# Second norm's channel weights moved from w_up to the normalised rows, the rows' scale given priority on GpSimd, and the values' two parts summed by one reduction from PSUM

## The chip, the cores and the metric

The kernel runs on one core of a Trainium2 chip. Its engines are TensorE (PE in the profile, with its weight loads as PEld), VectorE (DVE), ScalarE (ACT), GpSimd (POOL) and SyncE (SP), which issues the DMAs. The metric is the time of one execution in microseconds (us); a row's durations are in us unless marked ns.

## The reference

One layer of a hybrid decoder, on 1024 tokens of 1024 channels with 16 meta tokens ahead of them:

```python
def rms_norm(x, g):
    xf = x.astype(jnp.float32)
    y = xf * lax.rsqrt(jnp.mean(xf * xf, axis=-1, keepdims=True) + EPS)
    return (y * g.astype(jnp.float32)).astype(x.dtype)
...
        hn = rms_norm(h, norm1_gain[l])
        proj = jnp.einsum('bld,de->ble', hn, w_in[l])
...
        mixed = jnp.concatenate([attn_out, conv_out], axis=-1)
        h = h + jnp.einsum('ble,ed->bld', mixed, w_out[l])
        hn = rms_norm(h, norm2_gain[l])
        a = jax.nn.relu(jnp.einsum('bld,df->blf', hn, w_up[l]))
        h = h + jnp.einsum('blf,fd->bld', a * a, w_down[l])
    return h[:, N_META:]
```

`proj` holds queries, keys and values of 4 heads and the input of a convolution group. The attention is causal and differential: for each head `a = p[0] - lam * p[1]`, two softmax maps of 64-wide queries and keys, times values of 128 columns, and an RMS norm of each head's result. `w_up` is 1024 x 4096, `w_down` 4096 x 1024, all in float32.

## The kernel before

**Exact products out of parts.** Every float32 operand of a matrix product is split into a high part, rounded to fp32r, and a low part, the remainder. The helpers `split` and `halves` do it: ACT copies the high part, and DVE (or GpSimd, where `eng` says so) subtracts it from the source. `three` (L319 to L321) then makes a product of three matmuls, high x high, high x low, low x high. Nearly all of TensorE's work goes through it, so a line of the profile such as `px<-hnt,wp` is told by its tile.

**Stages.** From 0 to 20 us x is loaded, normalised and transposed; to 240 us the projections of the convolution, keys and queries run, with the convolution's taps on DVE; to 480 us the attention, the values, and the output product; to about 530 us the rest of the output product and the second norm; to 820 us the up stage; then the down stage.

**The attention's values.** `values(i, h, u)` runs for each of 8 tiles of 128 queries and 4 heads. For each block of keys, one matmul multiplies the weights' high part with the value's high and low part side by side (256 columns of a PSUM tile `ops`), and one adds the weights' low part times the value's high part to the left 128. The two halves of `ops` are then added: ACT copies the right one to `ob` (L623), DVE adds the left one to it, into `osb` (L624).

**The second norm.** `attn_out` adds the output product to the residual into `hs` (or `h2k`, for the tiles that stay in SBUF) and sums its squares. When both halves of a tile of 128 rows are there, two GpSimd operations make the row's scale: `ms` (L698, sum and epsilon) and `rs2` (L699, power -1/2; `rs` in the profile). `normed(t)` multiplies the rows by that scale on DVE (`xn`, L832), 512 columns at a time, and TensorE transposes them into PSUM (`htr`, L835). The channel weights of the norm are not applied there but to the rows of `w_up` when these are loaded (`wload`): by ACT for each load of 128 x 4 x 256 (L894, four instructions), by GpSimd for the first eight, of 128 x 4 x 128 (L892). They lie in SBUF as `gains`, one column for each block of 128 channels.

**The up stage.** It multiplies blocks of 2 x 2 with seven products in place of eight. So the transposed rows are needed in seven forms: `hn11`, `hn21`, `hn22` and the sums and differences `hnt1` to `hnt4`, made by `norm_first`, `norm_second` and `norm_third`, the last in halves of 256 columns (`hnt` in the profile; `scr` and `hraw` hold what they are made of). The weights have seven forms too, made by `up_prep(g)`: sums `s1`, `s2` on DVE out of two loads `wr`, then parts `wp`. `group(g)` runs for 16 blocks of 256 columns of `w_up`; in it `snap` copies a product from PSUM to `sn` on ACT (L941), after which TensorE goes on accumulating into the same bank. The first four groups begin early, while the norm still runs: `up_early` multiplies `hn11` and `hn21` with parts made by `prep_early`, whose low parts GpSimd makes. 

**What sets the order.** The program is written out by hand; a scheduler then orders the instructions of each engine by the program's order, its own model of times and the priorities (`tc.high_priority`). An engine works through its own list in order. All DMAs of the lines below are issued on SP's queue, in order as well.

Of the kernel before, what the change touches and what calls it, by code (L numbers as in the profile page):

```python
# [9 lines left out]
F32 = mybir.dt.float32  # L10
# [49 lines left out]
def hybrid_layer_kernel(  # L60
# [36 lines left out]
    def small(shape, name, bufs=2):  # L97
        return sp.tile(shape, F32, tag=name, name=name, bufs=bufs)
# [62 lines left out]
    xm = cp.tile([P, 8, 48], F32R, tag="xm", name="xm")  # L161
# [67 lines left out]
    V.tensor_scalar(gsub, cvec[:, 0, 3:4], (1.0 - 0.2) * P ** 0.5, None, ALU.mult)  # L229

# [381 lines left out]
    def values(i, h, u):  # L612
# [10 lines left out]
        S.activation(ob, ops[:, P:2 * P], AF.Copy)  # L623
        V.tensor_tensor(out=osb[:, h, :], in0=ops[:, 0:P], in1=ob, op=ALU.add)  # L624
# [59 lines left out]
    def attn_out(pool, t, nh, keep=None):  # L684

        if keep is None:
            hs = tmp([P, 512], F32, "hs")
        else:
            hs = keep.tile([P, 512], F32, tag="ut", name="h2k", bufs=UT)
            h2t.setdefault(t, []).append(hs)  # L690
        nc.sync.dma_start(hs, cvo[t, nh])
        ps = half_out(pool, ma, state[0, nh], t)
        V.tensor_tensor(out=hs, in0=hs, in1=ps, op=ALU.add)
        nc.sync.dma_start(h2d[t][:, 512 * nh:512 * nh + 512], hs)
        S.activation(ps, hs, AF.Square, scale=D ** -0.5, accum_out=ssq[:, t, nh:nh + 1])
        if nh:
            ms = small([P, 8], "ms", 4)[:, :1]
            G.tensor_scalar(ms, ssq[:, t, 0:1], ssq[:, t, 1:2], EPS, ALU.add, ALU.add)  # L698
            G.tensor_tensor(out=rs2[:, t:t + 1], in0=ms, in1=mhalf[:, :1], op=ALU.pow)  # L699
# [51 lines left out]
    for n in range(-1, len(units) + BLAG):  # L751
# [12 lines left out]
        if n == 1:  # L764
            st_pool.__exit__(None, None, None)
            yt_pool.__exit__(None, None, None)
            aux_pool = tc.tile_pool(name="aux", bufs=1, side="right", reuse_waits="tile")
# [53 lines left out]
    def normed(t):  # L821
# [8 lines left out]
        for kf in range(2):  # L830
            xn = sp.tile([P, 512], F32, tag="raw", name="xn", bufs=4)
            V.tensor_scalar(xn, hv[kf], rs2[:, t:t + 1], None, ALU.mult)  # L832
# [34 lines left out]
    def norm_third():  # L867

        for name in ("t4", "t1", "t3"):
            operand(name)  # L870
            for c in (256, 0):
# [6 lines left out]
                elif name == "t1":  # L878
                    halves(hi, lo, t1)
# [7 lines left out]
    def wload(g, j, n):  # L887
# [3 lines left out]
        if n == P:  # L891
            G.tensor_tensor(out=r, in0=r, in1=gains[:, 1, 4 * j:4 * j + 4].unsqueeze(2).broadcast_to([P, 4, P]), op=ALU.mult)  # L892
        for k in range(4) if n > P else ():
            S.activation(r[:, k, :], r[:, k, :], AF.Copy, scale=gains[:, 1, 4 * j + k:4 * j + k + 1])  # L894
# [204 lines left out]
    up_pool.__exit__(None, None, None)  # L1099
    ps_c.__exit__(None, None, None)  # L1100
# [136 lines left out]
```

## Time and profile before

| what | value |
|---|---|
| median of 3 runs | 1135.59 us (1133.06 to 1140.71) |
| profiled execution | 1135.33 us, span 1133.2 us |
| PE | 1098.8 us busy, 97% of the span |
| DVE | 817.2 us, 72% |
| ACT | 617.1 us, 54% |
| POOL | 149.2 us, 13% |

The span is the time from the first to the last instruction in the trace; the profiled execution's time is measured around it. A busy share counts an engine's instructions over the whole span. It doesn't say which engine is waited for: that is read from the waits, the idle time of an instruction just before it starts and what ended it. The granted clock (PEclk) is the share of its full speed that TensorE had; 0.5 is the lower of its two levels, 1.2 GHz, and 1.0 the upper, 2.4 GHz.

### The profile page before, as it was taken

How to read it: one execution, taken by the hardware profiler on the slowest of the kernel's cores; microseconds unless marked ns; L12 is line 12 of the kernel's file. 1: busy time of each engine (PE TensorE's matmuls, PEld its weight loads, DVE VectorE, ACT ScalarE, POOL GpSimd, SP SyncE). 2: the span in 40 equal slices, each digit the busy share in tenths (PEclk: the TensorE clock that was granted, in tenths of full speed). 3: DMA queues.
4: the chain of work that ended last, by engine and by line, in shares of the span. 5: the costliest groups of instructions: out<-in, count | busy, mean ns of one | idle time of the engine just before them, and what ended most of it. 6: DMA issues, size and time to landing. Idle time of an engine off the chain costs nothing.

```text
span 1133.2 us, 15762 instructions
## 1 busy us (share of the span) xinstructions
PE 1098.8 (97%) x5696; PEld 925.5 (82%) x5696; DVE 817.2 (72%) x1354; ACT 617.1 (54%) x1378; POOL 149.2 (13%) x160
## 2 busy tenths in 40 slices
PE   6999999999999999898999999999999999999998
PEld 6999788877788887786888877888878888888887
DVE  7699899977888788689688868787656545356340
ACT  7521465447667677568767667767555333323320
POOL 3000564313001351261000000000000000000000
PEclk9999999999999999998999999999999999999999
DMA  7420011100213411365489989879399675565600
GB/s 266 121 76 1 1 38 38 29 10 19 75 66 103 131 66 66 122 224 170 154 309 330 323 277 343 320 251 339 125 336 380 251 258 212 197 227 201 221 38 37
DMA packets 89309, 191.23 MB, mean 169 GB/s; under 512 B 7552, under 2 KB 28288, under 8 KB 83600
## 3 DMA queue, kind: packets, MB, share of 16 engines
q1 hardware_dynamic: 89232, 190.24, 48.0%
q8 instruction: 44, 0.72, 0.3%
q14 instruction: 33, 0.27, 0.1%
HBM read 130.44 MB, written 59.77 MB: 168 GB/s over the span
## 4 chain that ended last, share of the span: by engine, by line
PE 72%; DVE 10%; DMA 8%; ACT 5%; issue 3%; POOL 1%; SPq 0%; DVEq 0%; ACTq 0%; POOLq 0%
PE py L319 6%; PE py L320 6%; PE py L321 6%; PE px L321 5%; PE px L319 5%; PE px L320 5%; DMA wr<-in_w_up 3%; PE pu L319 3%; PE pu L320 3%; PE pu L321 3%; DMA wdr<-in_w_down 3%; PE pq L320 3%; PE pq L319 3%; PE pq L321 3%; PE ops L620 2%
## 5 line engine op out<-in xcount | busy, mean ns | idle before, releaser
L809 DVE TENSOR_TENSOR pair<-rv,pair 128x2048 fp32r<-128x2048 f32 x56 | 127.0, 2289 | 112.0 <-ACT pair L808 111.8
L808 ACT ACTIVATE pair<-rv 128x2048 fp32r<-128x2048 f32 x56 | 105.2, 1911 | 163.2 <-PE py L321 77.9
L319 PE MATMUL py<-pair 128*128 128x512 f32 x256 | 99.6, 389 | 0.0
L320 PE MATMUL py<-pair 128*128 128x512 f32 x256 | 99.6, 389 | 0.0
L321 PE MATMUL py<-pair 128*128 128x512 f32 x256 | 99.6, 389 | 0.0
L319 PE MATMUL px<-pair 128*128 128x512 f32 x192 | 74.8, 390 | 1.0 <-ACT pair L808 1.0
L320 PE MATMUL px<-pair 128*128 128x512 f32 x192 | 74.7, 389 | 0.0
L321 PE MATMUL px<-pair 128*128 128x512 f32 x192 | 73.8, 390 | 0.2 <-DVE pair L809 0.2
L320 PE MATMUL pu<-xT,w 128*128 128x260 f32 x256 | 72.4, 286 | 0.0
L321 PE MATMUL pu<-xT,w 128*128 128x260 f32 x256 | 71.7, 285 | 0.0
L319 PE MATMUL pu<-xT,w 128*128 128x260 f32 x256 | 71.7, 286 | 0.0
L894 ACT ACTIVATE wr<-wr,gains 128x256 f32<-128x256 f32 x128 | 55.0, 498 | 30.6 <-DMA wr<-in_w_up 29.7
L945 ACT ACTIVATE a<-a 128x512 f32<-128x512 f32 x60 | 36.9, 626 | 35.9 <-DVE a L812 24.6
L321 PEld LDWEIGHTS py<-pair 128*128 128x128 f32 x256 | 48.1, 188 | 10.0
L319 PEld LDWEIGHTS py<-pair 128*128 128x128 f32 x256 | 48.1, 188 | 9.9
L320 PEld LDWEIGHTS py<-pair 128*128 128x128 f32 x256 | 48.1, 188 | 9.9
L319 PE MATMUL px<-hnt,wp 128*128 128x512 f32 x128 | 50.5, 395 | 3.9 <-ACT sn L941 3.9
L321 PE MATMUL pq<-w,xT 128*128 128x512 f32 x128 | 50.9, 398 | 0.0
L319 PE MATMUL pq<-w,xT 128*128 128x512 f32 x128 | 50.9, 397 | 0.0
L320 PE MATMUL pq<-w,xT 128*128 128x512 f32 x128 | 50.8, 397 | 0.0
L320 PE MATMUL px<-hnt,wp 128*128 128x512 f32 x128 | 50.4, 394 | 0.4 <-DVE hnt L809 0.4
L321 PE MATMUL px<-hnt,wp 128*128 128x512 f32 x128 | 50.5, 394 | 0.0
(301 smaller groups left out, 3197.6 us busy)
## 6 DMA issues: line engine op xcount, KB each, us to landing
rv<-as SPq DMA_DIRECT2D x28, 1024.0 KB, 6.3
wr<-in_w_up SPq DMA_DIRECT2D x32, 512.0 KB, 5.2
as<-a SPq DMA_DIRECT2D x64, 256.0 KB, 5.4
wdr<-in_w_down SPq DMA_DIRECT2D x8, 2048.0 KB, 9.5
ws<-wdr SPq DMA_DIRECT2D x32, 512.0 KB, 4.5
rv<-ws SPq DMA_DIRECT2D x16, 1024.0 KB, 4.8
as<-as SPq DMA_DIRECT2D x48, 256.0 KB, 4.1
rv<-in_w_down SPq DMA_DIRECT2D x12, 1024.0 KB, 6.6
```

What stands on the lines that cost most here:

```text
L319: T.matmul(ps, st[0], mv[0], start=first, stop=False, skip_group_check=more)
L320: T.matmul(ps, st[0], mv[1], start=False, stop=False, skip_group_check=more)
L321: T.matmul(ps, st[1], mv[0], start=False, stop=last, skip_group_check=more)
L620: T.matmul(ops, u[:, 0, b, :], vb.rearrange("p a e -> p (a e)"), start=b == 0, stop=False)
L808: S.activation(hi, src, AF.Copy)
L809: (eng or V).tensor_tensor(out=lo, in0=src, in1=hi.bitcast(F32), op=ALU.subtract)
L894: S.activation(r[:, k, :], r[:, k, :], AF.Copy, scale=gains[:, 1, 4 * j + k:4 * j + k + 1])
L945: S.activation(c, c, AF.Relu)
```

## The change

```diff
@@ -158,7 +158,7 @@
 
 
 
-    xm = cp.tile([P, 8, 48], F32R, tag="xm", name="xm")
+    xm = wpool[0].tile([P, 8, 48], F32R, tag="xm", name="xm", bufs=1)
     G.memset(xm.bitcast(F32), 0.0)
     mraw = slot([NMETA, D], F32, "mraw")
     nc.sync.dma_start(mraw, meta)
@@ -227,6 +227,10 @@
     V.tensor_scalar(lnh[:, 1, :], cvec[:, :, 2], 0.5, None, ALU.mult)
     gsub = cp.tile([P, 1], F32, tag="gsub", name="gsub")
     V.tensor_scalar(gsub, cvec[:, 0, 3:4], (1.0 - 0.2) * P ** 0.5, None, ALU.mult)
+
+
+    grow = dr.tile([8, P], F32, tag="grow", name="grow")
+    nc.sync.dma_start(grow.rearrange("k p -> p k"), gains[:, 1, :])
 
     gq = tmp([P, HD], F32, "gq")
     gk = tmp([P, HD], F32, "gk")
@@ -620,8 +624,7 @@
             T.matmul(ops, u[:, 0, b, :], vb.rearrange("p a e -> p (a e)"), start=b == 0, stop=False)
             T.matmul(ops[:, 0:P], u[:, 1, b, :], vb[:, 0, :], start=False, stop=b == i + 1)
         ob = ap.tile([P, P], F32, tag="ob", name="ob")
-        S.activation(ob, ops[:, P:2 * P], AF.Copy)
-        V.tensor_tensor(out=osb[:, h, :], in0=ops[:, 0:P], in1=ob, op=ALU.add)
+        V.tensor_reduce(osb[:, h, :], ops.rearrange("p (a e) -> p e a", a=2), axis=AX.X, op=ALU.add)
         S.activation(ob, osb[:, h, :], AF.Square, accum_out=oss[:, h:h + 1])
 
     def finish(i, osb, oss):
@@ -694,9 +697,10 @@
         nc.sync.dma_start(h2d[t][:, 512 * nh:512 * nh + 512], hs)
         S.activation(ps, hs, AF.Square, scale=D ** -0.5, accum_out=ssq[:, t, nh:nh + 1])
         if nh:
-            ms = small([P, 8], "ms", 4)[:, :1]
-            G.tensor_scalar(ms, ssq[:, t, 0:1], ssq[:, t, 1:2], EPS, ALU.add, ALU.add)
-            G.tensor_tensor(out=rs2[:, t:t + 1], in0=ms, in1=mhalf[:, :1], op=ALU.pow)
+            with tc.high_priority():
+                ms = small([P, 8], "ms", 4)[:, :1]
+                G.tensor_scalar(ms, ssq[:, t, 0:1], ssq[:, t, 1:2], EPS, ALU.add, ALU.add)
+                G.tensor_tensor(out=rs2[:, t:t + 1], in0=ms, in1=mhalf[:, :1], op=ALU.pow)
 
     uqs, pend = [], []
     for t in range(NT):
@@ -764,6 +768,9 @@
         if n == 1:
             st_pool.__exit__(None, None, None)
             yt_pool.__exit__(None, None, None)
+            gain_pool = tc.tile_pool(name="gain", bufs=1, side="right", reuse_waits="tile")
+            gain2 = gain_pool.__enter__().tile([P, D], F32, tag="gain2", name="gain2")
+            nc.sync.dma_start(gain2, grow.rearrange("k p -> (k p)").partition_broadcast(P))
             aux_pool = tc.tile_pool(name="aux", bufs=1, side="right", reuse_waits="tile")
             aux = aux_pool.__enter__()
             ap2 = tc.tile_pool(name="ap2", bufs=2, reuse_waits="tile")
@@ -829,7 +836,7 @@
         banks = []
         for kf in range(2):
             xn = sp.tile([P, 512], F32, tag="raw", name="xn", bufs=4)
-            V.tensor_scalar(xn, hv[kf], rs2[:, t:t + 1], None, ALU.mult)
+            V.scalar_tensor_tensor(xn, hv[kf], rs2[:, t:t + 1], gain2[:, 512 * kf:512 * kf + 512], ALU.mult, ALU.mult)
             bank = pcm.tile([P, 4, P], F32, tag="mm", name="htr")
             for q in range(4):
                 T.transpose(bank[:, q, :], xn[:, q * P:(q + 1) * P], ident)
@@ -876,7 +883,7 @@
                     sub(V, r21, t2, r21)
                     halves(hi, lo, r21)
                 elif name == "t1":
-                    halves(hi, lo, t1)
+                    halves(hi, lo, t1, G)
                 else:
                     sub(V, t2, t2, r11)
                     halves(hi, lo, t2)
@@ -888,10 +895,6 @@
 
         r = up.tile([P, 4, n], F32, tag="wr", name="wr", bufs=WRB, padded_shape=[P, 4, 256])
         nc.sync.dma_start(r, w_up[512 * j:512 * j + 512, 256 * g:256 * g + n].rearrange("(k p) f -> p k f", p=P))
-        if n == P:
-            G.tensor_tensor(out=r, in0=r, in1=gains[:, 1, 4 * j:4 * j + 4].unsqueeze(2).broadcast_to([P, 4, P]), op=ALU.mult)
-        for k in range(4) if n > P else ():
-            S.activation(r[:, k, :], r[:, k, :], AF.Copy, scale=gains[:, 1, 4 * j + k:4 * j + k + 1])
         return r
 
     def wpair(g, n, v, eng=None):
@@ -1097,6 +1100,7 @@
             next(run[g])
     next(run[NG - 1])
     up_pool.__exit__(None, None, None)
+    gain_pool.__exit__(None, None, None)
     ps_c.__exit__(None, None, None)
     tr_pool.__exit__(None, None, None)
```

Four things change. (a) The scaling of the loads of `w_up` by `gains` is gone from ACT and GpSimd. In its place `xn` is made by one SCALAR_TENSOR_TENSOR on DVE, with the row's scale and with `gain2`, a tile that holds the 1024 channel weights in each of the 128 partitions. `gain2` is loaded by one broadcasting DMA from `grow`, a row in DRAM, which an earlier DMA writes out of `gains`, transposing it. (b) The two GpSimd operations for the row's scale have a high priority. (c) The low parts of `hnt1` are made on GpSimd. (d) The two halves of `ops` are added by one TENSOR_REDUCE of DVE, which reads PSUM with the two values of a sum 128 columns apart; the copy `ob` on ACT goes (ACT still squares the result into it). `xm` moves to another pool.

GpSimd, the last operations that it has in the program, before; `wr` and `wp` are the early groups' loads and parts, `ms` and `rs2` the row's scale:

```order
L892 TENSOR_TENSOR wr_6294<-wr_6294,gains_106 128x4x128
L699 TENSOR_TENSOR rs2_2665<-ms_6191,mhalf_87 128x1
L892 TENSOR_TENSOR wr_6320<-wr_6320,gains_106 128x4x128
L892 TENSOR_TENSOR wr_6326<-wr_6326,gains_106 128x4x128
L809 TENSOR_TENSOR wp_6291<-wr_6288,wp_6291 128x512
L809 TENSOR_TENSOR wp_6297<-wr_6294,wp_6297 128x512
L698 TENSOR_SCALAR ms_6253<-ssq_2664 128x1
L809 TENSOR_TENSOR wp_6323<-wr_6320,wp_6323 128x512
L699 TENSOR_TENSOR rs2_2665<-ms_6253,mhalf_87 128x1
L809 TENSOR_TENSOR wp_6329<-wr_6326,wp_6329 128x512
```

And with the change:

```order
L816 TENSOR_TENSOR wp_6261<-wr_6259,wp_6261 128x512
L816 TENSOR_TENSOR wp_6266<-wr_6264,wp_6266 128x512
L702 TENSOR_SCALAR ms_6162<-ssq_2666 128x1
L703 TENSOR_TENSOR rs2_2667<-ms_6162,mhalf_87 128x1
L702 TENSOR_SCALAR ms_6224<-ssq_2666 128x1
L703 TENSOR_TENSOR rs2_2667<-ms_6224,mhalf_87 128x1
L816 TENSOR_TENSOR wp_6291<-wr_6289,wp_6291 128x512
L816 TENSOR_TENSOR wp_6296<-wr_6294,wp_6296 128x512
L816 TENSOR_TENSOR hnt1_6470<-scr_6165,hnt1_6470 128x4x256 x2
```

The scalings are gone, the last two pairs of `ms` and `rs2` stand together ahead of the last two parts, and the two halves of `hnt1` come at the end.

ACT in the up stage, around an `sn` of a group past the first four, before; `wr_7803` and `wr_7809` are the two loads from which this group's parts `wp` come, `wr_7983` is the second load of the next, `a11` and `a21` are results:

```order
L808 ACTIVATE wp_7815<-wr_7803 128x512
L946 ACTIVATE a11_7755<-a11_7755 128x512
L945 ACTIVATE a21_7771<-a21_7771 128x512
L946 ACTIVATE a21_7771<-a21_7771 128x512
L894 ACTIVATE wr_7983<-wr_7983,gains_106 128x256 x2
L941 ACTIVATE sn_7801<-px_7727 128x512
L808 ACTIVATE wp_7818<-wr_7809 128x512
L894 ACTIVATE wr_7983<-wr_7983,gains_106 128x256 x2
```

The same place with the change, where the group's own loads are `wr_7698` and `wr_7700`:

```order
L948 ACTIVATE a11_7650<-a11_7650 128x512
L949 ACTIVATE a11_7650<-a11_7650 128x512
L815 ACTIVATE wp_7702<-wr_7698 128x512
L948 ACTIVATE a21_7666<-a21_7666 128x512
L949 ACTIVATE a21_7666<-a21_7666 128x512
L944 ACTIVATE sn_7696<-px_7622 128x512
L815 ACTIVATE wp_7705<-wr_7700 128x512
L815 ACTIVATE wp_7712<-s2_7709 128x512
```

Two scalings of the next group's second load stood ahead of `sn` and two behind it. Now only results and a part made from the group's own first load stand ahead, and no instruction of this piece reads the next group's loads.

DVE at the end of the second norm, from the last pair of `xn`, before; `scr` and `hraw` lead to the parts of `hnt1`, `hnt2` and `hnt4`:

```order
L832 TENSOR_SCALAR xn_6422<-h2k_6217,rs2_2665 128x512
L832 TENSOR_SCALAR xn_6429<-h2k_6235,rs2_2665 128x512
L809 TENSOR_TENSOR hnt4_6512<-hraw_5914,hnt4_6512 128x4x256
L809 TENSOR_TENSOR hnt1_6519<-scr_6194,hnt1_6519 128x4x256
L812 TENSOR_TENSOR scr_6194<-htr_6411,scr_6194 128x4x128
L812 TENSOR_TENSOR scr_6194<-htr_6424,hraw_5914 128x4x128
L815 TENSOR_TENSOR s1_6376<-wr_6364,wr_6370 128x512
L812 TENSOR_TENSOR scr_6194<-htr_6431,scr_6194 128x4x128
L812 TENSOR_TENSOR s2_6377<-s1_6376,wr_6364 128x512
L812 TENSOR_TENSOR wr_6364<-wr_6364 128x4x128
L812 TENSOR_TENSOR hraw_5914<-scr_6194,hraw_5914 128x4x256
L815 TENSOR_TENSOR s1_6395<-wr_6383,wr_6389 128x512
```

And with the change:

```order
L839 SCALAR_TENSOR_TENSOR xn_6373<-h2k_6188,rs2_2667,gain2_3418 128x512
L839 SCALAR_TENSOR_TENSOR xn_6380<-h2k_6206,rs2_2667,gain2_3418 128x512
L819 TENSOR_TENSOR scr_6165<-htr_6278,scr_6165 128x4x128
L819 TENSOR_TENSOR hraw_5889<-scr_6165,hraw_5889 128x4x256
L816 TENSOR_TENSOR hnt2_6166<-scr_6165,hnt2_6166 128x4x128
L819 TENSOR_TENSOR scr_6165<-htr_6355,hraw_5889 128x4x128
L816 TENSOR_TENSOR hn22_6167<-htr_6278,hn22_6167 128x4x128
L819 TENSOR_TENSOR scr_6165<-scr_6165,hraw_5889 128x4x256
L816 TENSOR_TENSOR hnt4_6463<-hraw_5889,hnt4_6463 128x4x256
L819 TENSOR_TENSOR scr_6165<-htr_6362,scr_6165 128x4x128
L819 TENSOR_TENSOR scr_6165<-htr_6375,hraw_5889 128x4x128
L816 TENSOR_TENSOR wp_6339<-s2_6336,wp_6339 128x512
```

The part of `hnt1` is gone from behind the last `xn`, the sums `s1` and `s2` of the first early group have gone ahead of them, and in their place stand the sums of an earlier tile.

DVE in the up stage with the change, where the sums `s1_7874` and `s2_7875` read the next group's two loads directly; `as` are sums of the group's results:

```order
L816 TENSOR_TENSOR wp_7702<-wr_7698,wp_7702 128x512
L822 TENSOR_TENSOR as1_7670<-a21_7666,a22_7602 128x512
L822 TENSOR_TENSOR s1_7874<-wr_7864,wr_7866 128x512
L819 TENSOR_TENSOR as2_7671<-as1_7670,a11_7484 128x512
L819 TENSOR_TENSOR a21_7666<-a11_7484,a21_7666 128x512
L819 TENSOR_TENSOR s2_7875<-s1_7874,wr_7864 128x512
L819 TENSOR_TENSOR wr_7864<-wr_7864 128x4x128
L819 TENSOR_TENSOR as4_7672<-a12_7587,as2_7671 128x512
```

`s1_7874` stands behind the first of the group's four sums `as`; before, it stood behind the fourth and behind one part `wp`.

## Rows read from the trace of the kernel before

**Rows 1.** Windows by stage: from and to, us, busy time and instructions by engine, PEclk, DMA

```profile
20.00:240.00 220.00, 220.00 (x1380) 196.02 (x1379) 199.71 (x369) 90.58 (x389) 58.24 (x37) 1.00 0.15 44
240.00:480.00 240.00, 228.87 (x1443) 193.08 (x1442) 187.43 (x460) 165.29 (x428) 56.50 (x73) 1.00 0.22 75
480.00:530.00 50.00, 44.81 (x216) 36.72 (x216) 44.35 (x62) 37.68 (x78) 25.03 (x24) 0.93 0.62 205
530.00:820.00 290.00, 286.05 (x1253) 235.87 (x1252) 225.62 (x336) 201.62 (x393) 0.00 (x0) 0.99 0.79 276
```

**Rows 2.** Waits of TensorE: for which line, us in total, times, longest us

```profile
PE htr L835 <- DVE xn L832: 4.7, 2, 4.4
PE px L319 <- ACT sn L941: 3.9, 2, 2.8
...
PE ops L620 <- DVE osb L624: 1.2, 2, 0.7
```

**Rows 3.** Costliest groups of the page: busy us, mean ns, idle before and its releaser

```profile
L894 ACT ACTIVATE wr<-wr,gains 128x256 f32<-128x256 f32 x128 | 55.0, 498 | 30.6 <-DMA wr<-in_w_up 29.7
```

**Rows 4.** Timeline of ACT in the up stage: start, duration, then idle before

```profile
681.77 0.91 ACT L894 ACTIVATE wr<-wr,gains 128x256 f32<-128x256 f32 x2 [1.24 <-DMA wr<-in_w_up]
```

**Rows 5.** Timeline of TensorE at the same place

```profile
683.21 0.50 PE L319 MATMUL px<-hnt,wp 128*128 128x512 f32 x1 [2.79 <-ACT sn L941]
...
684.48 0.60 PE L321 MATMUL px<-hnt,wp 128*128 128x512 f32 x1
...
688.12 0.39 PE L321 MATMUL px<-hn,wp 128*128 128x512 f32 x1
```

**Rows 6.** GpSimd's groups by form between 489 and 528.1 us

```profile
L809 POOL TENSOR_TENSOR wp<-wr,wp 128x512 fp32r<-128x512 f32 x8 | 10.7, 1355 | 0.1
L892 POOL TENSOR_TENSOR wr<-wr,gains 128x512 f32<-128x512 f32 x8 | 8.5, 1075 | 8.5 <-PE htr L835 7.1 <-DVE hn L809 1.3
```

**Rows 7.** Timeline of GpSimd at the last tile of the norm

```profile
512.85 1.54 POOL L699 TENSOR_TENSOR rs<-ms,mhalf 128x1 f32<-128x1 f32 x1
```

**Rows 8.** Timeline of DVE from there to the last part of `hnt2`

```profile
514.49 1.81 DVE L832 TENSOR_SCALAR xn<-h2k,rs 128x512 f32<-128x512 f32 x2
...
526.24 1.81 DVE L809 TENSOR_TENSOR hnt<-scr,hnt 128x1024 fp32r<-128x1024 f32 x2
```

**Rows 9.** Timeline of TensorE in the second norm

```profile
504.22 1.03 PE L835 MATMUL htr<-ident,xn 128*128 128x128 f32 x8
505.01 0.48 PE L319 MATMUL px<-hn,wp 128*128 128x512 f32 x1
...
516.05 1.94 PE L835 MATMUL htr<-ident,xn 128*128 128x128 f32 x8 [4.41 <-DVE xn L832]
...
520.73 0.39 PE L320 MATMUL px<-hn,wp 128*128 128x512 f32 x1
...
528.11 0.51 PE L320 MATMUL px<-hnt,wp 128*128 128x512 f32 x1 [0.40 <-DVE hnt L809]
```

**Rows 10.** The `xn` of line 832: ns least/median/most; group between 489 and 528.1

```profile
L832 DVE TENSOR_SCALAR xn<-h2k,rs x8: 474/1258/1518, 489.0 to 515.8; 128x512 f32<-128x512 f32 x8
...
L832 DVE TENSOR_SCALAR xn<-h2k,rs 128x512 f32<-128x512 f32 x8 | 7.8, 1018 | 2.6 <-POOL rs L699 2.6
```

**Rows 11.** DVE's groups by form: a SCALAR_TENSOR_TENSOR of 512 columns

```profile
L139 DVE SCALAR_TENSOR_TENSOR w<-raw,gains,w 128x512 fp32r<-128x512 f32 x40 | 29.3, 744 | 1.1 <-ACT w L138 1.1
```

**Rows 12.** The values' copy and sum: ns least/median/most, first and last start

```profile
L623 ACT ACTIVATE ob<-ops x32: 258/277/303, 297.4 to 473.5; 128x128 f32<-128x128 f32 x32
...
L624 DVE TENSOR_TENSOR osb<-ops,ob x32: 258/282/292, 298.0 to 473.8; 128x128 f32<-128x128 f32 x32
```

**Rows 13.** DVE's groups by form: reductions of scores in PSUM

```profile
L578 DVE TENSOR_REDUCE mx<-sps 128x1 f32<-128x1024 f32 x8 | 9.6, 1216 | 1.3 <-PE sps L541 1.3
...
L578 DVE TENSOR_REDUCE mx<-sps 128x1 f32<-128x528 f32 x8 | 5.6, 696 | 1.4 <-PE sps L541 1.4
```

**Rows 14.** DMA issues: count, KB each, us from issue to landing

```profile
cvec<-in_cols SPq DMA_DIRECT2D x1, 8.0 KB, 6.0
```

## The prediction

> **What bounds the kernel now.** I read the windows by stage first, to see which engine has no time left. TensorE is busy for all 220 us of the projections, for 286.05 of 290 us in the up stage and for 228.87 of 240 us in the attention, but for only 44.81 of 50 us in the stretch of the second norm, at a mean granted clock of 0.93 [rows 1]. TensorE is the bound, so an edit pays only where TensorE stands still or runs at the lower clock. ACT and DVE have spare time in every stage as a whole; what they hold up must be looked for in TensorE's own waits, the second view. There the reader sees 4.7 us behind `xn`, 3.9 us behind `sn` and 1.2 us behind `osb` [rows 2]. These are the three places that the change touches.
>
> **a) The scaling of w_up on ACT goes.** 128 instructions of 55.0 us in sum, with 29.7 us of waiting for loads in front of them [rows 3], leave ACT. Most of it buys nothing, since TensorE does not wait for ACT there. It pays at two places. At 681.77 two scalings stand ahead of `sn` on ACT, the first after a wait of 1.24 us for the load of `wr` [rows 4]; TensorE waits 2.79 us for that `sn` [rows 5], and 1.1 us (3.9 less 2.8, rows 2) at a like place earlier. After the longer wait nine matmuls start within 3.64 us (684.48 to 688.12, rows 5). At the full clock matmuls are 286.05/1253 = 0.228 us apart [rows 1], so nine need 2.05 us, and 1.6 us are lost to the lower clock. That makes 1.1 + 2.8 + 1.6 = 5.5 us. In the new order nothing on ACT ahead of `sn` waits for that load. It is waited for on DVE, by `s1`, which has come up behind the first of the four sums `as`, with the other three and the parts `wp` behind it. The load had landed by 681.77; no row says when DVE will be there. I take -5.5, with no new wait; the bounds are -6 (also the clock behind the shorter wait) and 0 (the wait comes back on DVE).
>
> **b) The second norm.** The rows' scale `rs` is made by two small GpSimd operations for each tile, and for the last tile they stand among the long ones: `rs` comes at 512.85, right behind a low part, and takes 1.54 [rows 7]. DVE's last pair of `xn` starts at 514.49 [rows 8], and TensorE waits 4.41 us for it. Then the eight transposes and seven matmuls from 516.05 to 520.73 take 4.68 us, where such a set takes 0.79 (504.22 to 505.01) and seven matmuls 7 x 0.228 [rows 9], 2.4 together. So 4.4 + 2.3 = 6.7 us are lost, and 0.4 more behind `hnt` at 528.11: together 7.1.
>
> With `rs` ahead of the long operations the 6.7 us go at this place. But the next thing is late too. TensorE would come to the last part of `hnt2` at 528.1 - 6.7 = 521.4, and DVE writes that part at 528.05 (the pair at 526.24 lasts 1.81, rows 8). So DVE's work from the first `xn` at 489.0 [rows 10] to there decides: 39.0 us for 43 instructions. I price them from start to start, which is some 0.08 us below the durations listed, since the next starts before the last has ended: 0.40 for a TENSOR_SCALAR (0.474 listed at the least, rows 10), 0.60 and 1.14 for a TENSOR_TENSOR of 512 and 1024 columns (out of the 1.81). Step by step:
> - Eight `xn` become SCALAR_TENSOR_TENSOR, 0.744 listed where 0.48 was [rows 11]: 8 x 0.26 = +2.1.
> - The low parts of `hnt1`, two of 1.14, go to GpSimd: -2.3. The order puts two more operations of 0.60 into this stretch: +1.2.
> - Waiting for `rs` ends: -2.6 [rows 10].
> - The eight `xn` have 7.8 us in sum [rows 10] where 8 x 0.48 = 3.8: DVE is slowed while GpSimd works. Over the whole stretch I estimate 7.1 us: 39.0 less 4.5 idle, less 27.4 (8 x 0.40 + 6 x 1.14 + 29 x 0.60). GpSimd's long work in it goes from 10.7 + 8.5 = 19.2 us [rows 6] to about 16: the eight low parts, and two halves of `hnt1` at 2.6 each (twice as many columns). In proportion: 7.1 to 5.9, -1.2.
>
> 39.0 + 2.1 - 2.3 + 1.2 - 2.6 - 1.2 = 36.2, from a start about 1.1 later (eight earlier `xn`, +0.26 each, half of it in idle time): `hnt2` is ready at 526.3. TensorE then waits 4.9 us and loses 1.6 (as in a) to 2.3 us (as here) to the clock behind such a wait. I take 6.6 where 7.1 was lost: **-0.5**. Bounds: -7.1 (no wait at all, rival 1) and +3.4 (GpSimd stops DVE, rival 3).
>
> The Trainium skill ("SBUF — State Buffer", Who interferes with whom) says that DVE in its two-port mode, or with two inputs in SBUF, and GpSimd reading SBUF shut each other out of a shared port for a whole instruction. The trace agrees that there is such a thing: 474 ns at the least, 1258 at the median for the same `xn`. By that rule the new `xn`, with two inputs in SBUF, is not free of it, and the moved `hnt1` is a further collision, which is rival 3.
>
> **c) The values.** For each of 32 heads and tiles an ACT copy of 277 ns and a DVE sum of 282 ns [rows 12] give way to one reduction from PSUM. The trace has that operation only along contiguous rows: 1216 ns for 1024 columns, 696 for 528 [rows 13], which is 1.05 ns a column and 0.14 us fixed, so 0.41 us for 256 columns. DVE gets +0.13 x 32 = +4.1 us, ACT -8.9, and the chain to `osb` is 0.277 + 0.282 - 0.41 = 0.15 shorter, about 0.3 with the handover. TensorE waits for `osb` at two places today, 1.2 us [rows 2]. Bounds: -1.2 (these waits go) and +4.1 (all of the DVE time lands on the path). DVE is busy for 187 of 240 us there [rows 1], so the added time has cover, and I take -0.6 (0.3 at each of the two). How the reduction reads two values that lie 128 columns apart no row shows; if at half the rate, rival 4.
>
> **d) The gains as a row.** The transposing store writes 1024 pieces of 4 bytes, issued on SP's queue between `cw` and the next loads of x. `cvec`, 8 KB in 128 pieces, takes 6.0 us to land [rows 14]. I take 1.4 us of delay for the loads behind the store (eight sets of 128 pieces at under 0.2 us each, an estimate) and 0.5 of it at TensorE, since TensorE has work without gaps from 20 us on [rows 1] and can lose only before. Bounds: 0 and 6.0 (the loads wait out a whole landing). The broadcast load of `gain2` is issued where SP is idle, some 200 us ahead of its first reader, which covers any landing above: 0.
>
> **Sum.** -5.5 - 0.5 - 0.6 + 0.5 = -6.1 against the profiled execution's 1135.33 (the span of 1133.2 and 2.1 around it), which stands 0.3 below the median of the runs: 1129.2, rounded **1129**.
>
> **The rivals.**
> 1. *The norm pays in full.* `hnt2` comes before TensorE does. For it: `rs` is early, `hnt1` is off DVE, and without any slowing 36.2 - 5.9 puts `hnt2` at 520.4. Against: it needs every slowing that the rows show to be gone. b = -7.1: 1122.6, and 1121 with the low bounds of a, c and d. Chance 0.2.
> 2. *The load wait moves.* DVE works in order, `s1` waits for a load that ACT waited for, and behind it stand `wp` and the sums out of PSUM that TensorE needs. For it: 29.7 us of load waits [rows 3]. Against: few of them reach TensorE now. a = 0: 1134.7, and 1139 with the upper bound of c. Chance 0.22.
> 3. *GpSimd stops DVE.* Each half of `hnt1` blocks DVE for its 2.6 us: 36.2 + 5.2 - 1.9 (their share of the 5.9) = 39.5, `hnt2` at 529.6, 10.5 us lost where 7.1 were: b = +3.4, 1133.1. Chance 0.1.
> 4. *The other side: the reduction is slow.* At 2.1 ns a column it takes 0.68 us, +0.40 x 32 = +12.8 on DVE. If all of it lands on TensorE: 1129.2 + 0.6 + 12.8 = 1142.6. It decides where it eats the 5.5 us of the other parts: from 0.282 + 5.5/32 = 0.45 us a reduction if all lands, 0.63 if half does. Chance 0.08.
>
> **How the numbers follow.** My forecast (1126 to 1132) has the other 0.4, and 1129 is its time. The range 1119 to 1139 takes in rival 1 with its bounds, and 2 us below for the spread of a median, and rivals 2 and 3; outside lie most of rival 4 and the edges of the others, about 0.15. About 1% (11.4 us) is what a measurement of this kernel can tell from no change. Faster than 1124.2 is nearly all of rival 1 and a small tail of the forecast: 0.22. Slower than 1147 is only a part of rival 4 with something else: 0.04. The rest is 0.74.
>
> **What would show it.** a: no wait of TensorE behind `sn`, and none behind `s1` or `wp` in its place. b: `rs` ahead of the low parts on GpSimd, no wait at `htr`, but one of about 5 us behind `hnt`, and a granted clock near 0.93 again in that stretch; if the wait is missing, rival 1 holds. c: reductions of about 0.41 us; 0.68 would be rival 4. d: TensorE's first matmuls at the same time as before. I am wrong if DVE's work ahead of `hnt2` is shorter or longer than I sum it, or if a load that ACT waited for is late for DVE.

## The result, and the profile after

The changed kernel takes 1141.01 us (median of 10 runs, 1139.46 to 1144.77), the kernel before 1134.21 (10 runs). The ratio is 1.0063, with a 95% interval of 1.0047 to 1.0080: it is slower, by some 7 us, where 5 to 6 us less were forecast, and it lies 2 us above the range. The profiled execution took 1143.2 us, its span is 1141.4, 8.2 longer than the one before. One run of number 6 below, 1219.95 us at a granted clock of 0.852, is left out of its ratio.

Five marks on TensorE, read from both traces, tell in which stretch the time went. Between two neighbouring marks TensorE has the same number of matmuls in both kernels. The table has the start of an instruction in us; the last column is what the stretch that ends there added.

| TensorE's | before | after | difference | added in the stretch |
|---|---|---|---|---|
| first transpose of the third tile of x | 14.5 | 18.9 | +4.4 | +4.4 |
| first product of the values | 293.8 | 299.6 | +5.8 | +1.4 |
| last product of the values | 473.3 | 480.9 | +7.7 | +1.9 |
| last transpose of the second norm | 517.6 | 523.7 | +6.1 | -1.6 |
| first product of the down stage | 823.0 | 831.3 | +8.3 | +2.2 |

So there is a loss at the start, a smaller one in the attention, a gain up to the end of the second norm, and a loss behind it, although the waits of the up stage were to go there. TensorE's waits after (for which line, us in total, times, longest), beside [rows 2]:

```profile
PE xtr L190 <- DVE xs L185: 4.4, 1, 4.4
PE px L323 <- ACT wp L815: 4.0, 1, 4.0
...
PE px L323 <- ACT sn L944: 2.0, 2, 1.1
PE htr L842 <- DVE scr L819: 1.8, 1, 1.8
PE ops L624 <- DVE osb L627: 1.8, 2, 1.1
...
PE htr L842 <- DVE xn L839: 1.1, 2, 0.6
```

The wait of 4.4 us behind the last `xn` is gone, as forecast; the last transposes wait 1.8 us for `scr` instead. Two new waits of about the same length have come, 4.4 us at the start of the program and 4.0 behind the norm, and `sn` is waited for still. The windows by stage (columns as in [rows 1]):

```profile
240.00:480.00 240.00, 228.71 (x1429) 192.26 (x1428) 192.34 (x454) 156.26 (x387) 52.83 (x67) 0.99 0.21 69
480.00:530.00 50.00, 46.50 (x239) 38.30 (x240) 43.42 (x61) 28.07 (x64) 21.97 (x23) 1.00 0.72 240
530.00:552.00 22.00, 17.78 (x65) 13.70 (x64) 19.35 (x25) 11.99 (x20) 2.39 (x1) 0.84 0.34 113
552.00:820.00 268.00, 265.93 (x1171) 219.21 (x1170) 211.16 (x318) 151.76 (x267) 0.00 (x0) 1.00 0.82 286
```

ACT is busy for less time in each of these stages than in [rows 1], and TensorE as a whole is no faster for it. The stretch at the lower clock has moved from behind 513 us, within the norm, to behind 536 us; from 530 to 552 us the granted clock is 0.84 on the mean.

**The start.** DMA issues (KB each, us from issue to landing), the loads of x before:

```profile
xs<-in_x SPq DMA_DIRECT2D x8, 512.0 KB, 6.6
```

And after:

```profile
xs<-in_x SPq DMA_DIRECT2D x8, 512.0 KB, 11.7
...
cvec<-in_cols SPq DMA_DIRECT2D x1, 8.0 KB, 10.7
...
grow<-gains SPq DMA_DIRECT2D x1, 4.0 KB, 11.8
```

The store of the gains, 4 KB in 1024 pieces, takes 11.8 us, and what is under way beside it takes longer: the loads of x 11.7 us at the median where they took 6.6, `cvec` 10.7 where it took 6.0 [rows 14]. ACT gets its next tile of x late, and TensorE with it (timelines of ACT and TensorE):

```profile
16.94 1.06 ACT L182 ACTIVATE junk<-xs 128x1024 bf16<-128x1024 f32 x1 [4.33 <-DMA xs<-in_x]
```

```profile
18.90 1.33 PE L190 MATMUL xtr<-ident,xs 128*128 128x128 f32 x5 [4.38 <-DVE xs L185]
```

**Behind the norm.** The two halves of `hnt1` on GpSimd, and what DVE does meanwhile (timelines of GpSimd and DVE):

```profile
522.53 1.28 POOL L816 TENSOR_TENSOR wp<-wr,wp 128x512 fp32r<-128x512 f32 x1 [5.42 <-ACT wp L815]
524.42 2.82 POOL L816 TENSOR_TENSOR hnt<-scr,hnt 128x1024 fp32r<-128x1024 f32 x1 [0.61 <-ACT hnt L815]
531.10 2.39 POOL L816 TENSOR_TENSOR hnt<-scr,hnt 128x1024 fp32r<-128x1024 f32 x1 [3.86 <-ACT hnt L815]
```

```profile
523.17 0.68 DVE L816 TENSOR_TENSOR hn<-htr,hn 128x512 fp32r<-128x512 f32 x1
...
524.90 3.42 DVE L816 TENSOR_TENSOR hnt<-hraw,hnt 128x1024 fp32r<-128x1024 f32 x1
528.24 0.68 DVE L819 TENSOR_TENSOR scr<-htr,scr 128x512 f32<-128x512 f32 x1
...
531.24 2.79 DVE L816 TENSOR_TENSOR hnt<-scr,hnt 128x512 fp32r<-128x512 f32 x1
```

A part that takes 1.21 us elsewhere (542.24 in the same timeline) lasts 3.42. It begins 0.48 us after GpSimd's half and ends 1.08 after that half has ended at 527.24, so nearly all of its 1.21 us of work comes after GpSimd is through. The next one, 0.68 elsewhere, lasts 2.79 and ends 0.54 after GpSimd's second half. The operation at 523.17, beside a GpSimd part as well, isn't stretched; one of its inputs lies in PSUM. This is rival 3. It is also the rule of the Trainium skill ("SBUF — State Buffer", Who interferes with whom) on two inputs in SBUF: the trace agrees, in what is held up, in what is not and in how long. DVE has no idle time from there to 535.8 us, so both delays, 2.2 and 2.1 us, 4.3 in all, come through to the sum `s2` of the second early group, at 535.15, and by it to TensorE (timelines of ACT and TensorE):

```profile
535.95 0.63 ACT L815 ACTIVATE wp<-s 128x512 fp32r<-128x512 f32 x1 [3.47 <-DVE s L819]
```

```profile
536.63 0.79 PE L323 MATMUL px<-hnt,wp 128*128 128x512 f32 x1 [4.03 <-ACT wp L815]
537.60 0.79 PE L323 MATMUL px<-hn,wp 128*128 128x512 f32 x1 [0.18 <-ACT s L974]
...
543.31 0.40 PE L325 MATMUL px<-hnt,wp 128*128 128x512 f32 x1
```

Behind the wait, 13 matmuls take from 537.60 to 543.31, 5.7 us where 13 x 0.228 = 3.0 are normal: 2.7 lost to the clock.

**The up stage.** The load that ACT waited for is waited for by DVE (timelines of DVE, ACT and TensorE at one of two such places):

```profile
764.28 0.69 DVE L822 TENSOR_TENSOR s<-wr 128x512 f32<-128x512 f32 x1 [3.33 <-DMA wr<-in_w_up]
764.88 0.68 DVE L822 TENSOR_TENSOR a<-sn,pw 128x512 f32<-128x512 f32 x1
```

```profile
765.60 0.63 ACT L948 ACTIVATE a<-a 128x512 f32<-128x512 f32 x1 [3.67 <-DVE a L822]
766.26 0.63 ACT L949 ACTIVATE a<-a 128x512 f32<-128x512 f32 x1
766.80 0.58 ACT L944 ACTIVATE sn<-px 128x512 f32<-128x512 f32 x1
```

```profile
767.43 0.50 PE L323 MATMUL px<-hnt,wp 128*128 128x512 f32 x1 [1.14 <-ACT sn L944]
```

`s` waits 3.33 us for its load, the sum behind it in DVE's order is late, ACT squares that sum before it comes to `sn`, and TensorE waits 1.14 us. That is rival 2, at a smaller size: 2.0 us behind `sn` in all, where 3.9 were before [rows 2], and no lower clock behind them.

**The values.** The reduction takes what was estimated (ns least, median, most):

```profile
L627 DVE TENSOR_REDUCE osb<-ops x32: 407/416/426, 301.9 to 481.2; 128x128 f32<-128x256 f32 x32
```

### The profile page after: what moved, and what is told of

Same layout as the page of the kernel before. It is cut to its first block, busy times and chain, and to the rows that moved or that the text cites. A ratio compares the mean times of both kernels' runs of the same rounds, so it can differ in the third digit from the quotient of the medians.

```text
span 1141.4 us, 15640 instructions
## 1 busy us (share of the span) xinstructions
PE 1101.9 (97%) x5696; PEld 926.4 (81%) x5696; DVE 827.7 (73%) x1352; ACT 562.4 (49%) x1218; POOL 144.9 (13%) x154
## 4 chain that ended last, share of the span: by engine, by line
PE 73%; DVE 10%; DMA 9%; ACT 4%; issue 2%; POOL 1%; SPq 0%; DVEq 0%; ACTq 0%; POOLq 0%
PE px L325 6%; PE px L324 6%; PE px L323 6%; PE py L324 6%; PE py L325 6%; PE py L323 6%; DMA wr<-in_w_up 3%; PE pu L323 3%; PE pu L325 3%; PE pu L324 3%; PE pq L323 3%; PE pq L324 3%; PE pq L325 3%; PE ops L624 2%; DMA wdr<-in_w_down 2%
## 5 line engine op out<-in xcount | busy, mean ns | idle before, releaser
L323 PE MATMUL px<-hnt,wp 128*128 128x512 f32 x128 | 50.6, 395 | 6.1 <-ACT wp L815 4.0
L819 DVE TENSOR_TENSOR wdr<-wdr 128x1024 f32<-128x1024 f32 x32 | 39.0, 1218 | 22.0 <-DMA wdr<-in_w_down 21.9
L815 ACT ACTIVATE wp<-wr 128x512 fp32r<-128x512 f32 x64 | 39.9, 628 | 26.1 <-PE pw L325 14.5
L324 PE MATMUL px<-hnt,wp 128*128 128x512 f32 x128 | 50.0, 391 | 0.0
```

Source lines behind the costliest of these rows:

```text
L323: T.matmul(ps, st[0], mv[0], start=first, stop=False, skip_group_check=more)
L324: T.matmul(ps, st[0], mv[1], start=False, stop=False, skip_group_check=more)
L815: S.activation(hi, src, AF.Copy)
L819: eng.tensor_tensor(out=out, in0=a, in1=b, op=ALU.subtract)
```

## The experiments

Each ratio is against the kernel before on the same chip, with its 95% interval. The changed kernel's own was 1.0063 [1.0047, 1.0080].

**1. The store late.** Of the changed kernel, with a true dependence, since the scheduler sets a store early that only stands late in the program:

```diff
-    nc.sync.dma_start(grow.rearrange("k p -> p k"), gains[:, 1, :])
...
+            V.tensor_copy(gcol[:, 0:1], l0s[:, 7, 0:1])
+            V.tensor_copy(gcol, gains[:, 1, :])
+            nc.sync.dma_start(grow.rearrange("k p -> p k"), gcol)
             nc.sync.dma_start(gain2, grow.rearrange("k p -> (k p)").partition_broadcast(P))
```

> The changed kernel with the transposing store of the gains moved from the start of the program to the attention, just ahead of the broadcast load that reads it. Theory 'store': the 1024 small pieces keep the DMA engines from the loads of x, and TensorE, which came 4.4 us late to the second half of x, never gets it back; this kernel starts as the one before and ends about 5 us earlier than the changed kernel, near 1136 us (ratio to before about 1.001). Rival 'swallowed': the lateness is made good by slack in the attention, and the time stays near 1141 (ratio 1.006).

Measured: 1137.87 us, ratio 1.0031 [1.0018, 1.0044]. TensorE's third tile of x starts at 14.2 us, its first product of the values 1.1 us ahead of the kernel before. The theory holds for the start; of the 5 us some 3 came off the time, and less in number 10, the same kernel again. The edit also changes the order of TensorE, DVE and ACT up to 232 us; number 8 keeps the changed kernel's.

**2. The low parts of `hnt1` on DVE.**

```diff
-                    halves(hi, lo, t1, G)
+                    halves(hi, lo, t1)
```

> The changed kernel with the low parts of hnt1 on DVE again. Theory 'block': in the changed kernel the two GpSimd parts of 2.8 and 2.4 us stretched one DVE part from 1.21 to 3.42 us and one from 0.68 to 2.79, 4.3 us in all; without them the DVE chain to the last part of hnt2 is 4.3 shorter and 2.3 longer, so TensorE's wait of 4.0 us falls to about 2 and the time by 2 to 4 us, to 1137 to 1139. Rival 'work': the wait comes from the longer xn on DVE, and putting work back on DVE makes it 2 us longer, near 1143.

Measured: 1138.24 us, ratio 1.0025 [1.0011, 1.0039], about 4 us by the ratios. TensorE's waits between 500 and 560 us come down to one, 1.6 us behind `scr`, and the clock is full from 530 to 552 us where it was 0.84 (from 520 to 530 us it is 0.83, half of what the changed kernel loses):

```profile
530.00:552.00 22.00, 22.00 (x98) 18.06 (x97) 20.80 (x30) 13.77 (x23) 0.00 (x0) 1.00 0.54 168
```

'Block' holds, 'work' is out.

**3. The values summed as before.**

```diff
-        V.tensor_reduce(osb[:, h, :], ops.rearrange("p (a e) -> p e a", a=2), axis=AX.X, op=ALU.add)
+        S.activation(ob, ops[:, P:2 * P], AF.Copy)
+        V.tensor_tensor(out=osb[:, h, :], in0=ops[:, 0:P], in1=ob, op=ALU.add)
```

> The changed kernel with the values summed as before, a copy on ACT and a sum on DVE. Theory 'reduction': the reduction of 0.416 us in place of 0.282 puts up to 4.3 us on DVE, and TensorE lost about 2.5 us more in the attention than before; without it the time falls to about 1138.5. Rival 'no matter': DVE's time has cover there, the loss comes from the shifted start, and the time stays at 1141.

Measured: 1144.63 us, ratio 1.0080 [1.0061, 1.0099]. Neither theory's time came. It isn't faster, so the reduction is not the main part of what the changed kernel lost; that it is slower is not clear, for the intervals overlap, and its profiled execution was 5.6 us late at the third tile of x where the changed kernel's was 4.4.

**4. All three undone.** Left are the channel weights on the rows, and the row scale's place.

> All three at once: store late, hnt1 on DVE, values as before; what is left of the change is the channel weights on the rows and the row scale ahead on GpSimd. If the three theories hold and add up: 1141 - 5 - 3 - 2.5 = 1130.5, below the kernel before (1134.2), since the waits of the up stage behind sn (5.5 us) are gone. If the up stage had gained nothing: 1134 or more.

Measured: 1131.78 us, ratio 0.9972 [0.9956, 0.9987]: faster than the kernel before, by about 3 us where 3.7 were expected. Its trace has no wait of 4 us at the start nor behind the norm, and 3.2 us behind `sn`.

**5. The reduction alone, in the kernel before.** The edit of 3 the other way round.

> The kernel before with one edit, the values' two halves summed by one reduction from PSUM. Theory 'cover': the reduction's longer DVE time (0.416 against 0.282 us) has cover in the attention and its shorter chain pays a little, so 1133 to 1135 (ratio 0.999 to 1.000), in line with the older sum having brought the changed kernel nothing (1144.6 in place of 1141.0). Rival 'load': DVE's added 4.3 us land on TensorE, 1137 to 1139 (ratio 1.003 to 1.004).

Measured: 1135.09 us, ratio 1.0007 [0.9992, 1.0022]: nothing that can be told. The trace is finer. From the first to the last product of the values TensorE takes 180.3 us, where the two profiles of the kernel before have 179.5 and 179.0, at the full clock in all three: about 1 us longer. All other profiles with the full clock in that stretch agree in the sign: 180.9 to 181.9 us in the changed kernel and numbers 1, 2 and 10, which have the reduction, and 179.1 in number 12, which has not. The rows are those of `ops` (first and last start), with the reduction and before:

```profile
L620 PE MATMUL ops<-vm,u x32: 331/366/389, 293.2 to 473.1; 128*128 128x256 f32 x32
L621 PE MATMUL ops<-vs,u x144: 218/222/308, 293.6 to 473.5; 128*128 128x128 f32 x144
```

```profile
L620 PE MATMUL ops<-vm,u x32: 279/365/390, 293.8 to 472.8; 128*128 128x256 f32 x32
L621 PE MATMUL ops<-vs,u x144: 218/222/306, 294.3 to 473.3; 128*128 128x128 f32 x144
```

**6. Store and `hnt1` undone, the reduction kept.**

> The changed kernel with the store of the gains late and the low parts of hnt1 on DVE; the reduction stays. With the three undone the time was 1131.8. Theory 'cover': the reduction costs nothing or pays a little, 1130 to 1132 (ratio 0.996 to 0.998). Rival 'load': with the reduction in, it is 2 to 4 us slower, 1134 to 1136.

Measured: 1132.98 us, ratio 0.9989 [0.9976, 1.0002]: 1 to 2 us slower than with the old sum (0.9972), with intervals that overlap. Between 'cover' and 'load', nearer to the first: by the runs and the traces together the reduction costs 1 to 2 us, and it gives nothing.

**7. `hnt1` on GpSimd alone, in the kernel before.** The edit of 2 the other way round.

> The kernel before with one edit, the low parts of hnt1 on GpSimd. Theory 'block': each part of some 2.6 us holds up a DVE operation with two inputs in SBUF until it ends, and TensorE waits behind the norm: 2 to 6 us slower, 1137 to 1140 (ratio 1.002 to 1.005), with two DVE operations stretched by about 2 us each. Rival 'overlap': DVE is relieved of 2.3 us and goes on beside GpSimd, 1132 to 1134.

Measured: 1134.57 us, ratio 1.0001 [0.9984, 1.0018]. No loss of the 2 to 6 us expected, so 'block' as a price is wrong here, though the blocking is there. GpSimd's first half falls beside the last `xn`, and TensorE's wait for it is 5.51 us where it was 4.41 [rows 9] (timelines of GpSimd, DVE, TensorE):

```profile
516.90 2.35 POOL L809 TENSOR_TENSOR hnt<-scr,hnt 128x1024 fp32r<-128x1024 f32 x1
```

```profile
517.03 3.91 DVE L832 TENSOR_SCALAR xn<-h2k,rs 128x512 f32<-128x512 f32 x2
...
525.00 2.90 DVE L812 TENSOR_TENSOR wr<-wr 128x512 f32<-128x512 f32 x1
```

```profile
519.68 1.09 PE L835 MATMUL htr<-ident,xn 128*128 128x128 f32 x4 [5.51 <-DVE xn L832]
```

The second half stretches a difference of weights at 525.00, and behind it TensorE waits only 1.6 us, for a part `wp`. From the last product of the values to the last transpose this kernel needs 46.3 us, where the kernel before has 44.3 and 43.7; from there to the down stage 302.7, where it has 305.4 and 305.6. So what is lost ahead of the last transpose is gained behind it. What the blocking costs goes by the operation that it meets. That need not have two inputs in SBUF: this `xn` is a TENSOR_SCALAR of one tensor, 0.474 us at the least [rows 10], and the pair took 3.91.

**8. An early store of 128 pieces.** The order of all engines stays that of the changed kernel; only the transposing store moves, as in 1:

```diff
-    nc.sync.dma_start(grow.rearrange("k p -> p k"), gains[:, 1, :])
+    gflat = dr.tile([P, 8], F32, tag="gflat", name="gflat")
+    nc.sync.dma_start(gflat, gains[:, 1, :])
...
```

> The changed kernel with the early store kept at its place and in the order of all engines, but writing the gains as they lie, 128 pieces of 32 bytes; the transposing store comes late, in the attention. Theory 'pieces': the 1024 pieces cost the start its 5 us, so this is near the kernel with the store late, 1137 to 1138.5 (ratio 1.002 to 1.003), and TensorE's first transposes of the third tile of x start near 14.5 to 15.5 us in place of 18.9. Rival 'order': the delay comes from the order of the loads and of TensorE's work that goes with a store at this place, and it stays at 1141 and 18 us or more.

Measured: 1140.94 us, ratio 1.0052 [1.0038, 1.0066]. Both theories hold, each for a part. The pieces set the start: this store takes 5.3 us, the loads of x 6.2, and the third tile of x starts at 14.7 us. But the time stays at 1141. At the first product of the values this kernel is within 1 us of number 1; at the last it is 2.7 us behind, and it falls back further behind the norm. In the trace the difference in the attention is two stretches at the lower clock, which number 1 does not have, although from 232 us on the two kernels have the same order on every engine.

**9, 10 and 11. The same three once more,** to see whether these stretches belong to the program.

> The kernel with the early store of 128 pieces once more, beside the kernel with the store late on the same chip. In the one profile of each, both start alike (TensorE 1.1 us ahead of the kernel before at the end of the projections), but the first lost 3.3 us to two stretches at the lower clock in the attention, after 284 and after 470 us, the second none. Theory 'program': these stretches go with the program, and this kernel is 2 to 3 us slower than the one with the store late again (1140 to 1141), with both stretches in its profile. Rival 'chance': they fall differently in each execution, the profile shows other places, and the two medians lie within 1.5 us.

> The kernel with the store late once more. Theory 'program': no stretch at the lower clock in the attention, 1137 to 1138. Rival 'chance': one or two such stretches in the attention, or the median within 1.5 us of the kernel with the early store of 128 pieces.

> The kernel before once more, for its profile: its first had no stretch at the lower clock in the attention, though TensorE waited 1.74 us at 285 us as in the others. Theory 'program': none again. Rival 'chance': one or two, of about 1.7 us each, and a span longer by as much.

Measured: the early store 1142.8 us, ratio 1.0072 [1.0050, 1.0093]; the store late 1139.42, ratio 1.0048 [1.0031, 1.0065]; the kernel before 1134.3 in one run. The first two medians are 3.4 us apart, and both lie above what was expected. The windows of two stretches of 10 us in the new profiles (the third figure from the end is the granted clock), of the early store and of the late one:

```profile
280.00:290.00 10.00, 8.26 (x36) 6.48 (x35) 7.66 (x19) 7.11 (x16) 0.00 (x0) 0.83 0.05 1
470.00:480.00 10.00, 9.32 (x40) 7.57 (x41) 4.13 (x12) 2.58 (x12) 3.33 (x6) 0.83 0.27 86
```

```profile
280.00:290.00 10.00, 8.26 (x46) 6.45 (x45) 8.20 (x20) 7.42 (x16) 0.00 (x0) 1.00 0.07 1
470.00:480.00 10.00, 9.32 (x48) 7.71 (x47) 4.85 (x12) 2.55 (x10) 3.74 (x6) 1.00 0.53 158
```

They are the same two places as in 8 (number 9 has two more stretches, behind 405 and 487 us), and there is none in either profile of the store late nor of the kernel before. So these six profiles of three kernels fit 'program'. The other traces don't. Up to 518 us number 6 has the order of numbers 1 and 10 on every engine, and yet two such stretches:

```profile
400.00:410.00 10.00, 8.47 (x55) 7.66 (x54) 7.30 (x13) 8.25 (x24) 8.29 (x8) 0.83 0.26 79
470.00:480.00 10.00, 9.16 (x41) 7.28 (x40) 4.54 (x14) 3.27 (x15) 2.58 (x6) 0.83 0.29 96
```

In the same way number 4 has a stretch behind 468 us and number 12 none, and number 7 has one behind 469 us and the kernel before none, each pair in the same order up to there. So the stretch near 470 us comes and goes with the execution. The one behind 284 us goes with the early store in four of five profiles (behind 288 and 290 us where the start was late, and not in number 3), and none of the nine profiles without an early store has one. But it can't come from the order at that place alone, which numbers 1 and 8 share. Why isn't settled: TensorE waits 1.74 us for `msb` just ahead, at 284.3 to 285.4 us, in all six, and the clock falls behind it in two of them. So it also stays open what the 3.4 us between the two medians consist of.

**12. The sums ahead of `s1`,** on top of number 4:

```diff
+        if prev:
+            V.tensor_copy(s1[:, 0, 0:1], prev[-1][:, 0:1])
         add(V, s1, l21, l22)
...
+        prev.append(a21)
```

> The kernel with the three parts undone (1131.8 us), and s1 held back on DVE until the group's last sums are done, by a copy of one column of a21 into s1 ahead of it (13 more small DVE instructions). Theory 'load wait': in the up stage DVE waits 8.9 us for loads in s1, and the sums behind it make sn late, for which TensorE waits 3.2 us; with s1 behind the sums these waits go, 1128 to 1130 (ratio 0.994 to 0.996), no wait of TensorE behind sn over 0.5 us. Rival 'parts late': held back, s1 and s2 make the parts wp late, and TensorE waits for these: 1132 or more.

Measured: 1132.79 us, ratio 0.9987 [0.9965, 1.0009], not to be told from number 4. Both theories hold a part: no wait behind `sn` is left in the up stage, and one of 2.8 us behind a part `wp` has come (TensorE's waits between 525 and 822 us):

```profile
PE px L322 <- ACT wp L820: 2.8, 1, 2.8
```

## Why the prediction was wrong, step by step

**d, the start: the size failed.** The forecast put 1.4 us of delay and 0.5 of loss where its bounds were 0 and 6.0. The step that failed is the scaling from `cvec`, eight sets of 128 pieces at under 0.2 us each, a price that no row shows: the store takes 11.8 us, the loads beside it take 5 us longer, and TensorE was 4.4 us late in the profiled execution (2.0 and 5.6 in numbers 2 and 3, with the same start). That work without gaps from 20 us on limits the loss, as was said, isn't so: the delay was 4.8 us at 100 us and 5.1 at the end of the projections, so none of it was made good. By the ratios, the store late gives back 3.6 us of it in number 1 (1.0031 for 1.0063) and 1.7 in number 10 (1.0048). Number 8 shows that the price isn't the pieces alone: with few pieces at the same place the start is on time, and about the same time is lost later, in part at the lower clock. What the early store does to that later time stays open.

**b, the second norm: the case was chosen wrongly.** What the change says it does, it does. `rs` has become early, DVE waits 0.2 us for it where it was 2.6 [rows 10], and the wait at the last `htr` has fallen from 4.4 to 1.8 us, now behind `scr`. (That `rs` comes first is not the priority's doing: without it every engine's order is the same; it follows from the scalings having left GpSimd.) The next wait behind the norm is there too, but behind `wp`, by the sum `s2`, and not behind the last part of `hnt2`, to which DVE's work was summed. With it TensorE loses 9.6 us in this stretch: 1.1 behind `xn`, 1.8 behind `scr`, 4.0 behind `wp` and 2.7 to the clock. The forecast had 6.6 and rival 3 had 10.5, where 7.1 were lost before, and 0.3 behind an earlier `xn`. Rival 3 priced this at +3.4 and 1133 in all; taking `hnt1` off GpSimd in number 2 gives 4 us. The failed step is the scaling of DVE's slowing with GpSimd's busy time (7.1 to 5.9 us). Slowing is no share of that time: the two operations of DVE with two inputs in SBUF that met a half of `hnt1` stood until it ended. So what counts is which operation is met and who waits for it. Number 7 has the same edit in another order, where what it costs at one place it gives back at the next. The eight `xn` cost less than feared, 8.1 us where they had 7.8 [rows 10] and +2.1 were summed: each has the term of +0.26, but only three met a part on GpSimd, at 1.2 to 1.8 us, where five did before (the group, and ns least, median, most):

```profile
L839 DVE SCALAR_TENSOR_TENSOR xn<-h2k,rs,gain 128x512 f32<-128x512 f32 x8 | 8.1, 1057 | 0.2 <-POOL rs L703 0.2
L839 DVE SCALAR_TENSOR_TENSOR xn<-h2k,rs,gain x8: 736/742/1775, 498.0 to 519.4; 128x512 f32<-128x512 f32 x8
```

**a, the up stage: right in kind, too large.** The 3.9 us behind `sn` fell to 2.0; the 2.0 are rival 2: DVE waits at `s1` for loads, 11.5 us in all. So the step that failed is "no new wait": part of the load wait has come back on DVE. The 1.6 us of lower clock was counted as if it came each time; the second profile of the kernel before has none at that place. From the last transpose of the norm to the down stage, numbers 2, 4 and 6, without the `hnt1` on GpSimd, need 301.8, 301.9 and 303.0 us, the kernel before 305.4 and 305.6: -2.4 to -3.8 for a with what b leaves, where a alone was to give -5.5.

**c, the values: the time of the operation was right, its effect not.** 0.416 us against the estimate of 0.41. The step that failed is the cover: DVE's added 4.3 us have less of it than thought, and the shorter chain pays nothing that shows: about +1 to +2 in the attention, not -0.6. Rival 4's half rate is out.

**Together**, in the profiled execution: +5.1 by the end of the projections, +2.6 in the attention (0.7 up to the first product of the values, with a stretch between 290 and 300 us at a granted clock of 0.83 in it, and 1.9 from there to the last, at the full clock), -1.6 up to the last transpose, and +2.2 behind it (307.6 us to the down stage; 302.2 on the mean of numbers 2, 4 and 6, so +5.4 for `hnt1`, and 305.4 before, so -3.2 for the up stage). That is 8.3, where the spans are 8.2 apart. The shares of the attention are read from one profile. Each part lies within its own bounds; the range took the rivals one at a time, and here the losses of d, b and c and a smaller gain of a came together.

## What to carry to other kernels

A small transfer of many tiny pieces at the start of a kernel delays the loads beside it, and a delay ahead of a bound engine's gapless stretch goes through that stretch whole (here 5 us, over 220 us of projections); the row was read 277 us later, and could be made then. Work moved to an idle engine is not free when its operands lie in the memory that a busy one reads: look up, in the new order, which operation stands beside it and who waits for that one. The part of the change that paid was the channel weights on the rows alone (0.9972), and the parts that came along cost more than it gave. And one profile of each of two kernels doesn't tell whether a stretch at the lower clock belongs to one of them: look for two traces with the same order first.

## What the runs showed of the hardware that was not expected

- 1024 pieces of 4 bytes (4 KB) took 11.8 us at the start, and 11.4 (number 1) and 8.3 us (number 8) in the attention; 128 pieces of 32 bytes with the same bytes took 5.3 at the start.
- GpSimd's subtraction of 1024 columns (2.4 to 2.8 us) held up a DVE subtraction from SBUF to its own end, 1.21 to 3.42 and 0.68 to 2.79 us, but not one with an input in PSUM (0.68 beside a part of 1.28).
- The same wait of TensorE, 1.74 us at 284 to 285 us, was followed by a granted clock of 0.83 from 280 to 290 us in number 9 and of 1.00 in number 10, in the same order of instructions from 232 us on; from 470 to 480 us number 6 had 0.83 and number 10 had 1.00 in the same order from the start.
